# Softmax minus one-hot over 8192 rows: row-wise transfers, hand-placed semaphores, column numbers in PSUM, and middle blocks moved as two transfers of half the partitions

## The chip, the cores and the metric

The kernel runs on one core of a Trainium2 chip. A core has compute engines that run side by side, each with its own instruction queue: TensorE (PE), VectorE (DVE), ScalarE (ACT), GpSimd (POOL) and SyncE (SP). Data moves between HBM (the large memory, in which inputs and outputs lie) and SBUF (the on-chip memory of 128 partitions) by DMA; here SP and ACT issue the transfers, each on a queue of its own. PSUM is a second, small on-chip memory of 128 partitions. The engines wait for each other and for transfers by semaphores.

The metric is the device time of one execution, in microseconds, given as the median of ten runs. Lower is better.

## The reference

The input is 8 x 1024 rows of 8192 float32 logits and one label per row. The output is the gradient of the cross entropy: the softmax of each row, less one at the row's label.

```
logits_max = np.max(logits, axis=-1, keepdims=True)
exp_logits = np.exp(logits - logits_max)
softmax = exp_logits / np.sum(exp_logits, axis=-1, keepdims=True)
one_hot[batch_idx, seq_idx, labels] = 1.0
return (softmax - one_hot).astype(np.float32)
```

268 MB are read and 268 MB written. The arithmetic is a maximum, an exponential with its sum, a scaling, and a compare with a subtraction, each over all elements.

## The kernel before

The 8192 rows are taken as 64 tiles (T) of 128 rows, one row per partition (P). A tile is 128 x 8192 float32, 4 MB, 32 KB in each partition, and is worked on in place. The pool `io` has six such slots (SLOTS).

Ahead of the loop the labels are loaded by ACT's queue (line 44), turned into one label per partition by a cast on DVE (56) and a transpose on PE (58), and written twice by DVE (61), once for each half of the columns (HALF, 4096). GpSimd writes the column numbers 0 to 4095 as int16 into SBUF (`iota`, 46).

Each tile t goes through six steps:

- `load(t)`, line 65: one transfer on SP's queue. It waits until the slot is free, that is for the store of tile t-6.
- `row_max`, line 70, on DVE: the negated maximum of each row, `m`.
- `exponent`, line 75, on ACT: exp(x + m) in place, with the sum `s` of each row.
- `inverse`, line 80, on DVE: `r`, the reciprocal of `s`.
- `normalize`, line 86, on ACT: x times r, as two instructions of 4096 columns.
- `subtract`, line 91, on DVE: x less (column number equals label), as two instructions of 4096 columns. The second half compares with the label less 4096.

and then `store(t)`, line 97: one transfer on ACT's queue.

The order on each engine is that of the program text (`manual_schedule`); the framework places the semaphores. The loop, lines 103 to 112, is skewed: within iteration t, DVE runs the inverse of t, the maximum of t+1 and then the subtract of t, and ACT runs the exponent of t, issues the store of t-1, and scales t. So the subtract of t stands behind the maximum of t+1 on DVE, and the latter waits for the load of t+1. SP carries only loads, and runs ahead as far as slots are free. PE and GpSimd have nothing to do in the loop.

Of the kernel before, what the change touches and what calls it, by code (L numbers as in the profile page):

```python
# [1 line left out]

# [4 lines left out]

P = 128
HALF = 4096
SLOTS = 6  # L10


@with_exitstack
def kernel(
    ctx: ExitStack,
    tc: tile.TileContext,
    logits: bass.AP,
    labels: bass.AP,
    out: bass.AP,
):  # L20
    nc = tc.nc
    fp32 = mybir.dt.float32
    i32 = mybir.dt.int32
    i16 = mybir.dt.int16
    Act = mybir.ActivationFunctionType
    Alu = mybir.AluOpType

    x_nv = logits.flatten_outer_dims()
    o_nv = out.flatten_outer_dims()
    N, V = x_nv.shape  # L30
    T = N // P
    C = V // HALF
    lab_tp = labels.rearrange("a b -> (a b)").rearrange("(t p) -> t p", p=P)

    const = ctx.enter_context(tc.tile_pool(name="const", bufs=1))
    io = ctx.enter_context(tc.tile_pool(name="io", bufs=SLOTS))
    stats = ctx.enter_context(tc.tile_pool(name="stats", bufs=4))
    psum = ctx.enter_context(tc.tile_pool(name="psum", bufs=1, space=bass.MemoryType.PSUM))
    ctx.enter_context(tc.manual_schedule())

    lab_raw = const.tile([T, P], labels.dtype)
    nc.scalar.dma_start(out=lab_raw[:], in_=lab_tp)
    iota = const.tile([P, HALF], i16)
    nc.gpsimd.iota(iota[:], [[1, HALF]], base=0, channel_multiplier=0)  # L46
    ident = const.tile([T, T], fp32)
    nc.gpsimd.memset(ident[:], 0.0)  # L48
    nc.gpsimd.affine_select(  # L49
        out=ident[:], in_=ident[:], compare_op=Alu.not_equal, fill=1.0,  # L50
        base=0, pattern=[[-1, T]], channel_multiplier=1,
    )
    lab_f = const.tile([T, P], fp32)
    lab32 = lab_raw[:].bitcast(i32)
    step = mybir.dt.size(labels.dtype) // 4
    nc.vector.tensor_copy(out=lab_f[:], in_=lab32.rearrange("t (p s) -> t p s", s=step)[:, :, 0])  # L56
    lab_ps = psum.tile([P, T], fp32)
    nc.tensor.transpose(out=lab_ps[:], in_=lab_f[:], identity=ident[:])  # L58
    lab = const.tile([P, C, T], fp32)
    for c in range(C):  # L60
        nc.vector.tensor_scalar_add(out=lab[:, c, :], in0=lab_ps[:], scalar1=float(-c * HALF))  # L61

    def load(t):
        x = io.tile([P, V], fp32, tag="x", name="x")
        nc.sync.dma_start(out=x[:], in_=x_nv[t * P : (t + 1) * P, :])  # L65
        return x

    def row_max(x):
        m = stats.tile([P, 1], fp32, tag="m", name="m")
        nc.vector.tensor_reduce(out=m[:], in_=x[:], axis=mybir.AxisListType.X, op=Alu.max, negate=True)  # L70
        return m

    def exponent(x, m):
        s = stats.tile([P, 1], fp32, tag="s", name="s")
        nc.scalar.activation(out=x[:], in_=x[:], func=Act.Exp, bias=m[:], scale=1.0, accum_out=s[:])  # L75
        return s

    def inverse(s):
        r = stats.tile([P, 1], fp32, tag="r", name="r")
        nc.vector.reciprocal(out=r[:], in_=s[:])  # L80
        return r

    def normalize(x, r):
        for c in range(C):
            xc = x[:, c * HALF : (c + 1) * HALF]
            nc.scalar.activation(out=xc, in_=xc, func=Act.Copy, bias=0.0, scale=r[:])  # L86

    def subtract(t, x):
        for c in range(C):
            xc = x[:, c * HALF : (c + 1) * HALF]  # L90
            nc.vector.scalar_tensor_tensor(  # L91
                out=xc, in0=iota[:], scalar=lab[:, c, t : t + 1], in1=xc,
                op0=Alu.is_equal, op1=Alu.subtract, reverse1=True,
            )

    def store(t, x):
        nc.scalar.dma_start(out=o_nv[t * P : (t + 1) * P, :], in_=x[:])  # L97


    xs, ms = {}, {}  # L100
    xs[0] = load(0)
    ms[0] = row_max(xs[0])
    for t in range(T):
        s = exponent(xs[t], ms[t])
        r = inverse(s)
        if t + 1 < T:
            xs[t + 1] = load(t + 1)
            ms[t + 1] = row_max(xs[t + 1])
        if t > 0:
            store(t - 1, xs[t - 1])  # L110
        normalize(xs[t], r)
        subtract(t, xs[t])
    store(T - 1, xs[T - 1])


# [1 line left out]
_INS = ['logits', 'labels']  # L117
_OUTS = [((8, 1024, 8192), 'float32')]


# [23 lines left out]
```

## Time and profile before

| what | value |
|---|---|
| median of ten runs | 1248.19 us (1248.06 to 1248.61) |
| the profiled execution, its own time | 1248.27 us |
| span of its profile | 1246.4 us |
| load of a tile, issue to landing (median) | 24.2 us |
| store of a tile, issue to landing (median) | 54.9 us |
| maximum of a tile, DVE | 8680 ns |
| exponent of a tile, ACT | 7122 ns |
| scale of half a tile, ACT | 3700 ns |
| subtract of half a tile, DVE | 4476 ns |

The profile is of one execution. Its span is somewhat shorter than the time of the run, which holds what lies before the first and after the last recorded instruction. "Busy" of an engine counts its compute instructions. In the rows, "L70" is line 70 of the kernel, `m<-x` says that `m` is written from `x`, and a name after `<-` at the end of a row is what the engine waited for last. The time from issue to landing includes the time that a transfer stands in its queue behind earlier ones. q1 is the queue of SP's transfers and q10 that of ACT's.

### The profile page before, as it was taken

The numbers are of one execution on the slowest core, as the hardware profiler recorded it, in microseconds if no ns is written. First come the engines' busy times: TensorE is split into PE (matmuls) and PEld (weight loads), VectorE is DVE, ScalarE is ACT, GpSimd is POOL, SyncE is SP. The second block draws the span as 40 slices with busy tenths as digits, with TensorE's granted clock in tenths as the row PEclk, the third lists the DMA queues.
The fourth block names the chain that finished last, engine by engine and source line by source line (L and its number), as shares of the span: only waits on it lengthen the run. The fifth ranks groups of instructions, "written<-read, shape, count | busy, mean of one in ns | idle before, by whom it ended". The sixth has DMA issues, their size and how long they took to land.

```text
span 1246.4 us, 997 instructions
## 1 busy us (share of the span) xinstructions
PE 0.3 (0%) x1; PEld 0.2 (0%) x1; DVE 1122.1 (90%) x259; ACT 930.7 (75%) x257; POOL 4.1 (0%) x7
## 2 busy tenths in 40 slices
PE   0000000000000000000000000000000000000000
PEld 0000000000000000000000000000000000000000
DVE  3999999999988989889898898988989989899893
ACT  3888888888877777777777777677777777777772
POOL 1000000000000000000000000000000000000000
DMA  9999999999999999999999999999999999999998
GB/s 403 424 436 432 428 437 435 432 430 435 435 431 431 435 435 431 430 435 434 432 429 437 432 433 429 437 433 431 431 437 431 433 431 436 433 432 431 436 433 380
DMA packets 18519, 537.00 MB, mean 431 GB/s; under 512 B 2064, under 2 KB 2128, under 8 KB 2128
## 3 DMA queue, kind: packets, MB, share of 16 engines
q1 hardware_dynamic: 9216, 268.44, 50.0%
q10 hardware_dynamic: 9296, 268.51, 49.9%
q14 instruction: 7, 0.06, 0.0%
HBM read 268.50 MB, written 268.44 MB: 431 GB/s over the span
## 4 chain that ended last, share of the span: by engine, by line
another core or an unknown queue 66%; DVE 21%; DMA 7%; issue 3%; SPq 1%; ACT 1%; DVEq 0%; ACTq 0%
DVE m L70 11%; DVE x L91 10%; DMA out_dram<-x 4%; DMA x<-in_logits_dram 3%; SPq L65 1%; ACT x L75 1%; DVEq L139 0%; ACT x L86 0%; DVE r L80 0%; ACTq L97 0%; DVEq L91 0%; DVEq L70 0%
## 5 line engine op out<-in xcount | busy, mean ns | idle before, releaser
L70 DVE TENSOR_REDUCE m<-x 128x1 f32<-128x8192 f32 x64 | 555.5, 8680 | 84.0 <-DMA x<-in_logits_dram 83.9
L75 ACT ACTIVATE x<-x,m 128x8192 f32<-128x8192 f32 x64 | 455.8, 7122 | 157.2 <-DVE m L70 157.2
L91 DVE SCALAR_TENSOR_TENSOR x<-iota,lab,x 128x4096 f32<-128x4096 int16 x128 | 567.7, 4476 | 4.1 <-ACT x L86 4.1
L86 ACT ACTIVATE x<-x,r 128x4096 f32<-128x4096 f32 x128 | 467.6, 3700 | 123.5 <-DVE r L80 123.5
L80 DVE RECIPROCAL r<-s 128x1 f32<-128x1 f32 x64 | 9.9, 155 | 7.3 <-ACT x L75 7.3
L75 ACT ACTIVATION_READ_ACCUMULATOR x<-x,m 128x1 f32 x64 | 12.0, 187 | 0.0
L75 ACT ACT_TABLE_LOAD x1 | 1.3, 1283 | 13.6 <-DMA x<-in_logits_dram 13.6
L56 DVE CAST lab_f<-lab_raw 64x128 f32<-64x128 int32 x1 | 0.2, 219 | 12.3 <-DMA lab_raw<-in_labels_dram 12.3
L46 POOL IOTA iota<- 128x4096 int16 x1 | 3.5, 3540 | 0.4 <-POOLq L128 0.4
L61 DVE TENSOR_SCALAR lab<-lab_ps 128x64 f32<-128x64 f32 x2 | 0.4, 219 | 0.5 <-PE lab_ps L58 0.5
L58 PE MATMUL lab_ps<-ident,lab_f 64*128 64x64 f32 x1 | 0.3, 335 | 12.7 <-DVE lab_f L56 12.7
L49 POOL TENSOR_SCALAR_AFFINE_SELECT ident<-ident 64x64 f32<-64x64 f32 x1 | 0.2, 232 | 0.1
L58 PEld LDWEIGHTS lab_ps<-ident,lab_f 64*128 64x128 f32 x1 | 0.2, 177 | 12.6 <-issue 12.6
L48 POOL MEMSET ident<- 64x64 f32 x1 | 0.1, 144 | 0.0
L128 POOL MEMSET const-bfloat16-1.0<- 128x1 bf16 x1 | 0.1, 106 | 0.0
L128 POOL MEMSET const-uint8-127<- 128x1 uint8 x1 | 0.1, 106 | 0.0
L128 POOL MEMSET const-float32-0.0<- 128x1 f32 x1 | 0.1, 103 | 0.2 <-issue 0.2
L128 POOL MEMSET const-float32-1.0<- 128x1 f32 x1 | 0.1, 103 | 0.0
## 6 DMA issues: line engine op xcount, KB each, us to landing
x<-in_logits_dram SPq DMA_DIRECT2D x64, 4096.0 KB, 24.2
out_dram<-x ACTq DMA_DIRECT2D x64, 4096.0 KB, 54.9
lab_raw<-in_labels_dram ACTq DMA_DIRECT2D x1, 64.0 KB, 11.5
```

What stands on the lines that cost most here:

```text
L46: nc.gpsimd.iota(iota[:], [[1, HALF]], base=0, channel_multiplier=0)
L49: nc.gpsimd.affine_select(out=ident[:], in_=ident[:], compare_op=Alu.not_equal, fill=1.0, base=0, pattern=[[-1, T]], channel_multiplier=1,)
L56: nc.vector.tensor_copy(out=lab_f[:], in_=lab32.rearrange("t (p s) -> t p s", s=step)[:, :, 0])
L58: nc.tensor.transpose(out=lab_ps[:], in_=lab_f[:], identity=ident[:])
L61: nc.vector.tensor_scalar_add(out=lab[:, c, :], in0=lab_ps[:], scalar1=float(-c * HALF))
L65: nc.sync.dma_start(out=x[:], in_=x_nv[t * P : (t + 1) * P, :])
L70: nc.vector.tensor_reduce(out=m[:], in_=x[:], axis=mybir.AxisListType.X, op=Alu.max, negate=True)
L75: nc.scalar.activation(out=x[:], in_=x[:], func=Act.Exp, bias=m[:], scale=1.0, accum_out=s[:])
L80: nc.vector.reciprocal(out=r[:], in_=s[:])
L86: nc.scalar.activation(out=xc, in_=xc, func=Act.Copy, bias=0.0, scale=r[:])
L91: nc.vector.scalar_tensor_tensor(out=xc, in0=iota[:], scalar=lab[:, c, t : t + 1], in1=xc, op0=Alu.is_equal, op1=Alu.subtract, reverse1=True,)
L128: nc = _bacc.Bacc("TRN2", target_bir_lowering=False, num_devices=1)
```

## The change

A new layout of rows: 256 rows are a block, there are 32 blocks (B), and partition p holds rows 2p and 2p+1 of the block (G = 2, index j). So the two rows of a partition lie side by side in HBM, and in SBUF in the tile `X` of three block slots (SLOTS is now 3), as large as the six slots before. One step of the loop still handles 128 rows: row j of each partition.

A block moves in one of three ways, set for each block by the strings LOADS and STORES:

- `r`: two transfers, one for each j, each over all 128 partitions with 32 KB per partition;
- `h`: two transfers, the even partitions and the odd ones, each with both rows, 64 KB per partition;
- `w`: one transfer, all partitions with both rows.

Loads are `r` for block 0, `w` for block 1, `r` for 2 to 6, `h` for 7 to 26 and `r` to the end. Stores are `r` for blocks 0 to 3, `h` for 4 to 23, `r` for 24 to 29, `w` for 30 and `r` for 31. A load of block b waits for those stores of block b-3 that share elements with it. A maximum waits for all transfers that bring part of its row. With `h` or `w`, the store is issued after the second row of the block.

Loads stay on SP's queue and stores on ACT's. The semaphores are placed by hand: the helper `run` gives each instruction its last wait and puts any other wait ahead of it as an instruction of its own. Slots of loads and of stores have semaphores of their own, two per slot. At the end ACT waits for the last stores.

The column numbers 0 to 8191 are written by GpSimd as int16 into what will be the second row of slot 2, and copied by DVE, read as int32, into a PSUM tile[...]. The load of that row (block 2, j = 1) waits for the copy. The label transposes use the same PSUM tile before that. The scale and the subtract take a whole row in one instruction, except for the last tile, whose scale and subtract stay in halves. The order of steps on DVE and ACT in the loop is as before. The statistics `m`, `s` and `r` have a column for each tile instead of rotating buffers.

The diff, cut to its core:

```
-HALF = 4096
-SLOTS = 6
+G = 2
+SLOTS = 3
+LOADS = "rwrrrrrhhhhhhhhhhhhhhhhhhhhrrrrr"
+STORES = "rrrrhhhhhhhhhhhhhhhhhhhhrrrrrrwr"
...
+    x_b = x_nv.rearrange("(b p j) v -> b p j v", p=P, j=G)
+    o_b = o_nv.rearrange("(b p j) v -> b p j v", p=P, j=G)
...
+    X = const.tile([P, SLOTS, G, V], fp32)
...
+    iota = psum.tile([P, V], i16)
+    lab_ps = iota[:].bitcast(fp32)[:, :T].rearrange("p (j b) -> p j b", j=G)
...
+        def run(engine, waits, counter, method, **operands):
+            waits = list(dict.fromkeys(waits))
+            for w in waits[:-1]:
+                engine.wait_ge(*w)
+            instruction = getattr(engine, method)(**operands)
+            for w in waits[-1:]:
+                instruction._wait_ge(*w)
+            step = 16 if method == "dma_start" else 1
+            instruction.then_inc(counter, step)
...
+        made = X[:, SLOTS - 1, G - 1, :].bitcast(i16)[:, :V]
+        w_made = run(
+            nc.gpsimd, [], pool, "iota", out=made, pattern=[[1, V]], base=0, channel_multiplier=0
+        )
...
+        w_iota = run(
+            nc.vector, [w_turned, w_made], dve, "tensor_scalar",
+            out=iota[:].bitcast(i32), in0=made.bitcast(i32), scalar1=0, scalar2=None, op0=Alu.bitwise_or,
+        )
...
+        PIECES = {
+            "r": [(every, slice(j, j + 1)) for j in range(G)],
+            "h": [(slice(i, P, 2), rows) for i in range(2)],
+            "w": [(every, rows)],
+        }
...
+        def load(b):
+            loaded[b] = []
+            before = stored.get(b - SLOTS, last_made if b == SLOTS - 1 else [])
+            for q, piece in enumerate(PIECES[LOADS[b]]):
+                ps, js = piece
+                free = [w for other, w in before if meets(piece, other)]
+                w = run(
+                    nc.sync, free, got[b % SLOTS][q], "dma_start",
+                    out=X[ps, b % SLOTS, js, :], in_=x_b[b, ps, js, :],
+                )
+                loaded[b].append((piece, w))
+        def store(t):
+            b, j = divmod(t, G)
+            stored.setdefault(b, [])
+            for q, piece in enumerate(PIECES[STORES[b]]):
+                ps, js = piece
+                if js.stop != j + 1:
+                    continue
+                w = run(
+                    nc.scalar, [finished[t]], put[b % SLOTS][q], "dma_start",
+                    out=o_b[b, ps, js, :], in_=X[ps, b % SLOTS, js, :],
+                )
+                stored[b].append((piece, w))
...
+            n = 1 if t + 1 < T else 2
+            cols = [slice(i * V // n, (i + 1) * V // n) for i in range(n)]
...
+        store(T - 1)
+        for b in range(B - SLOTS, B):
+            for _, w in stored[b]:
+                nc.scalar.wait_ge(*w)
```

## The prediction

> **What bounds the kernel now.** I read the page first: part 1 for the engines, part 2 for the DMA row, part 3 for the queues, then the waits of the compute engines and of SP, then a table of stages, and last the timeline of one row in the middle and of the end.
>
> ```profile
> PE 0.3 (0%) x1; PEld 0.2 (0%) x1; DVE 1122.1 (90%) x259; ACT 930.7 (75%) x257; POOL 4.1 (0%) x7
> DMA  9999999999999999999999999999999999999998
> GB/s 403 424 436 432 428 437 435 432 430 435 435 431 431 435 435 431 430 435 434 432 429 437 432 433 429 437 433 431 431 437 431 433 431 436 433 432 431 436 433 380
> ...
> q1 hardware_dynamic: 9216, 268.44, 50.0%
> q10 hardware_dynamic: 9296, 268.51, 49.9%
> ```
>
> The sixteen DMA engines are busy in every slice, and queues q1 (loads) and q10 (stores) share their time half and half. VectorE is the next engine with 90%. Is it close enough to be the bound? The stages answer that (columns: stretch, its length, busy time and count of each engine, clock, DMA share, GB/s):
>
> ```profile
> 20.00:60.00 40.00, 0.00 (x0) 0.00 (x0) 32.72 (x9) 33.34 (x9) 0.00 (x0) 1.00 0.99 423
> 60.00:290.00 230.00, 0.00 (x0) 0.00 (x0) 230.00 (x54) 191.71 (x54) 0.00 (x0) 1.00 1.00 433
> 290.00:600.00 310.00, 0.00 (x0) 0.00 (x0) 283.76 (x67) 235.70 (x65) 0.00 (x0) 1.00 1.00 433
> 600.00:900.00 300.00, 0.00 (x0) 0.00 (x0) 272.15 (x62) 223.88 (x63) 0.00 (x0) 1.00 1.00 433
> ...
> 1230.00:1247.00 17.00, 0.00 (x0) 0.00 (x0) 0.25 (x1) 0.00 (x0) 0.00 (x0) 1.00 0.74 318
> ```
>
> From 60 to 290 us VectorE is full and eats the lead of the six loads that were issued at once. The DMA moves 433 GB/s there too, and goes on at 433 when VectorE falls back to 91%. So the rate doesn't depend on who waits for whom. The waits say the same from the other side:
>
> ```profile
> DVE m L70 <- DMA x<-in_logits_dram: 83.9, 46, 2.4
> ```
>
> and, in SP's own list,
>
> ```profile
> SPq L65 <- DMA out_dram<-x: 1149.3, 58, 67.1
> ```
>
> The row maximum waits for loads, and SP's loads wait for stores to free a slot. One row in the middle:
>
> ```profile
> 500.95 8.69 DVE L70 TENSOR_REDUCE m<-x 128x1 f32<-128x8192 f32 x1 [1.80 <-DMA x<-in_logits_dram]
> 509.55 8.87 DVE L91 SCALAR_TENSOR_TENSOR x<-iota,lab,x 128x4096 f32<-128x4096 int16 x2
> ...
> 518.45 0.34 ACTq L97 DMA_DIRECT2D out_dram<-x  x1
> ...
> 520.75 8.69 DVE L70 TENSOR_REDUCE m<-x 128x1 f32<-128x8192 f32 x1 [2.26 <-DMA x<-in_logits_dram]
> ```
>
> VectorE needs 8.69 + 8.87 + 0.16 (the reciprocal) = 17.7 us a row less overlaps, 17.45 in the full stretch. A row in and out is 8.39 MB, at 433 GB/s 19.37 us. All 536.9 MB at 433 are 1240 us of a span of 1246.4. Only 6.4 us lie outside the saturated rate: the start (403 and 424 GB/s in the first two slices) and the drain of the last store (380).
>
> [...] 9216 packets for 64 loads are 8192 data packets of 32 KB plus 16 small ones a transfer. At 433 a wave of sixteen 32 KB packets takes 1210.8 ns[...].
>
> **The change, part by part.**
>
> *Row-wise loads and stores (r) in 12 blocks.* The same 4 MB transfers of 128 pieces of 32 KB, only with a step of 64 KB in DRAM. The same count, the same size: 0. It is bounded below and above by a DRAM effect of the step that no row shows; I take 0, with 0.3% (1 us) either way.
>
> *Whole blocks and half partitions (w, h).* 20 blocks of loads and 20 of stores go as two transfers of 64 partitions, and one load and one store as one transfer of 128. The bytes are 42 of 64 blocks' worth, 65.6%, or 813 of the 1240 us. Two rows of one partition lie side by side in DRAM and in X, so a piece is 64 KB instead of 32 KB, if the DMA takes it whole. [...] If the piece is still cut at 32 KB it is nothing. [...] I take 1.9.
>
> *Fewer slots, coarser.* Three blocks of two rows instead of six rows: the same SBUF. But with h a row can begin only when both halves have landed, and both stores are issued only after the second row. The loop is: a block lands; its first maximum and the previous row's subtract follow; the store of the previous block is issued 17.5 us after the landing (500.95 to 518.45). Then store half 0, load half 0 beside store half 1, load half 1: 3 x 19.4 us while both queues are full. In all 75.7 us of the two block periods, 77.5. Before, the same loop had five row periods, 96.9, for 17.5 + 2 x 19.4 = 56.3. So 40 us of slack shrink to 1.8, and the hand-offs have to fit in there: a load takes 24.2 us from issue to landing by part 6 where its transfer takes 19.4, so 4.8 each. They don't fit. What then? A late load leaves the stores alone, which then go at 9.7 us a transfer instead of 19.4, so the lost time comes back. At full rate the loop is 17.5 + 3 x 9.7 + 3 x 4.8 = 61 us, under 77.5. The DMA loses only when both queues are empty at once. Stepped from a landing at 0, with the store of half 1 8.8 us of work short of its end beside the next load's half 0: shared, it ends at 17.6, the next store is issued at 17.5, and the load has about 1 us left. An idle DMA answers about 1 us after an issue: SP's first is at 0.74 us, and in the DMA view of the first 20 us the first bytes stand in the slice from 1.5 to 2.0. I take no gap. It rests on each half's load waiting for the store of the same half only.
>
> *Whole-row scale and subtract.* ACT's two of 3.70 become one, by the exponent's row (7.12) 0.2 us shorter; VectorE's two become one of about 8.75. The subtract now starts after the whole scale, not after its first half. In the middle the scale ends at 526.15 and the subtract can't start before 529.35, so the cover is 3.2 us; in the full stretch it is 0.8 us (54.75 against 55.59). Cost 0. The last row stays in halves.
>
> *Column numbers in PSUM.* The subtract reads 8192 int16 from PSUM. [...] The bound below is 0 gain; above, VectorE has 19.37 - 8.69 - 0.16 = 10.5 us for it before it becomes the bound. To fill it, VectorE copies 4096 int32 ahead of the first maximum: as long as a half subtract, about 4.4 us. The first maximum starts at 18 instead of 13.51, and the first store is issued at 51.5 instead of 47.04. What hides it is the loads, 25.2 MB, that alone last until about 60 us. Then the two first stores leave a hole of up to a microsecond around 72 us, as the second isn't issued before 69. I take 0.5, between 0 and 1.5.
>
> *Hand-placed semaphores.* Extra waits of half blocks stand on SP, before loads that wait for stores anyway, and on VectorE before a maximum: a few tens of ns against 1.8 us of idle. Behind that maximum wait the subtract and, through it, ACT's store; they waited there before. SP carries nothing but loads, so nothing else is held. 0. The waits at the end on ACT replace those of L139 (SP waits there for the last store): 0, up to 0.5 either way.
>
> Sum: -1.9 + 0.5 = -1.4 on the profiled run of 1248.27 us (span 1246.4 and 1.9 around it), 1246.9. The median, 1248.19, is the same within 0.1: 1246.8 us.
>
> **Rivals.**
> 1. [...] It decides from 0.5% (4 us) on. For it: nothing in before excludes it. [...] 0.13.
> 2. *Both queues run dry in the h loop.* A gap of 1 us per block is 20 us, 1267; 0.2 us decides. For it: the slack of 1.8 against hand-offs of 4.8. Against: the idle queue's answer and the full rate. 0.10, half of it below 1258.
> 3. *VectorE becomes the bound*, with a PSUM read slower by a fifth: each us over 10.5 costs 64 us. 1311. 0.02.
> 4. *The pieces are cut at 32 KB*: only the late start remains, 1248.7. It is in the main case's range.
>
> **How the numbers follow.** The main case, DMA saturated throughout, has 0.75, mostly from 1244.2[...] to 1249.5. A measurement can tell about 0.2%, 2.5 us, from no change. Of the 0.75 I put 0.30 below 1245.7, 0.41 within and 0.04 above 1250.7. With the rivals 0.29 is slower. The range leaves out rival 1, half of rival 2 and rival 3: 1244.2 to 1258; the likeliest case's own is 1244.2 to 1249.5.
>
> **What would show it.** Right: packets fall from 18519 to about 13000; the middle stages read 434 with a DMA share of 1.00; VectorE's subtract is one row of some 8.75 us; the first maximum starts near 18 us. Rival 1: share 1.00 but GB/s well under 433 in the middle only. Rival 2: a share under 1.00 there. Rival 3: VectorE full to the end. Wrong altogether: [...]a shorter start or drain, for which I see no cause.

## The result, and the profile after

The changed kernel takes 1276.61 us (median), the one before 1248.23 us. The ratio is 1.0227, with a 95% interval of 1.0216 to 1.0237: 28 us slower, where 1.4 us faster were forecast. Its runs also scatter more, 1272.9 to 1280.7 us; of the 29 runs before, all but two (1254.0 and 1280.6) lie within 0.8 us. The profiled execution took 1275.87 us with a span of 1273.9, against 1246.4 before.

First the lines of the page that answer to those read before: the DMA row, GB/s in 40 slices, the packets and the two queues.

```profile
DMA  9999999999999999999999999999999999999998
GB/s 397 427 429 437 433 430 444 420 430 430 397 397 428 428 422 430 399 428 428 395 432 391 428 428 424 428 391 430 428 399 426 425 415 430 437 432 429 439 443 372
DMA packets 13076, 536.98 MB, mean 422 GB/s; under 512 B 2032, under 2 KB 2032, under 8 KB 2064
...
q1 hardware_dynamic: 6512, 268.44, 50.4%
q10 hardware_dynamic: 6560, 268.51, 48.8%
```

The pieces did become 64 KB: 13076 packets instead of 18519. But in the middle, where the h blocks are, GB/s dips below 400 in seven slices (11, 12, 17, 20, 22, 27 and 30; a slice is 31.8 us), where before it never fell under 428 there. It comes back to 429 and more when the rows go one by one again (slices 34 to 39). The stages show the same, and what the DMA share says of it (columns as before):

```profile
60.00:290.00 230.00, 0.00 (x0) 0.00 (x0) 209.42 (x37) 173.51 (x37) 0.00 (x0) 1.00 1.00 431
290.00:600.00 310.00, 0.00 (x0) 0.00 (x0) 272.58 (x49) 223.33 (x49) 0.00 (x0) 1.00 0.99 419
600.00:900.00 300.00, 0.00 (x0) 0.00 (x0) 264.36 (x46) 218.47 (x46) 0.00 (x0) 1.00 0.99 416
900.00:1150.00 250.00, 0.00 (x0) 0.00 (x0) 228.72 (x40) 188.97 (x40) 0.00 (x0) 1.00 1.00 425
1150.00:1230.00 80.00, 0.00 (x0) 0.00 (x0) 71.43 (x14) 58.07 (x15) 0.00 (x0) 1.00 1.00 433
```

The rate falls by 3 to 4%, the busy share by only 1%. So engines stand idle a little, and are slow for the rest: two losses, not one. In the waits the maximum is held less often and much longer: 25 times and up to 20.2 us, where it was 46 times and at most 2.4 us.

```profile
DVE m L68 <- DMA X<-in_logits_dram: 106.6, 25, 20.2
ACT X L68 <- DVE r L68: 75.0, 44, 2.1
ACT X L68 <- issue: 73.7, 20, 6.4
```

What decides is in the chain of work that ended last. Its pieces between 563 and 686 us, in order of time (start, length, what):

```profile
563.52 41.66 DMA out_dram<-X
605.18 0.02 issue
605.20 21.52 DMA X<-in_logits_dram
626.72 0.02 issue
626.74 8.69 DVE m L68
635.43 7.32 DVE X L68
642.74 1.26 issue
644.00 0.17 DVE r L68
644.17 0.43 ACTq L68
644.60 0.04 issue
644.64 41.31 DMA out_dram<-X
685.95 0.02 issue
685.96 21.30 DMA X<-in_logits_dram
```

This is the loop of the prediction, closed: the stores of a block, the load into the freed half slot, the first maximum of the block that landed, the subtract of the row before, the next stores. A round takes 644.64 - 563.52 = 81.1 us and carries two blocks each way, for which the DMA needs 77.5 at 433 GB/s. It is the longest of seven in a row; they take 80.2 on average (by their store issues), 2.7 over, and ten such rounds, for 20 blocks, are 27 us. The chain of the kernel before can't be laid beside it: its pieces in the middle are put down to "another core or an unknown queue". The load at 605.20 is issued when the load before it is about to end and the stores have ended. The DMA view of 600 to 620 us (40 slices of half a microsecond) counts a packet where it starts, in both rows, so a 0 alone is no idle engine:

```profile
DMA  9900699006007993000994099990306933039030
GB/s 786 1180 0 0 262 1311 524 0 0 262 0 0 262 1311 393 131 0 0 0 1573 393 131 0 262 262 393 1049 0 131 0 262 1573 131 131 0 131 1835 0 131 0
```

The individual packet records of the trace say how many engines had a packet: 16 until 605.0, 2 at 606.0, 16 again from 607.75. As stages: 321 GB/s from 604 to 614 us, with a share of 0.92. The records also give the two losses a size. A 64 KB packet takes 2.418 us (two of 32 KB took 2 x 1.213), and nine in ten are within 0.1 us of that. The exceptions come in bursts: from 200 to 1050 us, packets that took longer than their kind add 21.6 us to each engine's time, nearly all of them loads (20.1). Most of it comes in eight bursts of some 32 packets (two per engine on average), each of which costs an engine 1.8 to 2.3 us on average, always right behind a load's restart like that at 605; the rest in smaller ones. Engines without a packet add 7.5 us. Together 29.1 us, less 2.7 that the larger packets save (8 ns on each of 5376, spread over 16 engines), against a span longer by 27.5.

### The profile page after: what moved, and what is told of

The parts are those of the page before. It is cut to its first block, busy times and chain, and to the rows that moved or that the text cites. A ratio compares the mean times of both kernels' runs of the same rounds, so it can differ in the third digit from the quotient of the medians.

```text
span 1273.9 us, 629 instructions
## 1 busy us (share of the span) xinstructions
PE 0.4 (0%) x2; PEld 0.3 (0%) x2; DVE 1117.6 (88%) x196; ACT 917.9 (72%) x194; POOL 7.4 (1%) x7
## 2 busy tenths in 40 slices
DMA packets 13076, 536.98 MB, mean 422 GB/s; under 512 B 2032, under 2 KB 2032, under 8 KB 2064
## 3 DMA queue, kind: packets, MB, share of 16 engines
q10 hardware_dynamic: 6560, 268.51, 48.8%
## 4 chain that ended last, share of the span: by engine, by line
DMA 61%; DVE 34%; ACT 1%; issue 1%; ACTq 1%; DVEq 0%; PE 0%; SPq 0%
DMA out_dram<-X 38%; DMA X<-in_logits_dram 23%; DVE m L68 17%; DVE X L68 16%; ACT X L68 1%; ACTq L68 1%; DMA lab_raw<-in_labels_dram 0%; DVE iota L68 0%; DVEq L56 0%; DVE r L68 0%; DVE lab_f L68 0%; PE iota L68 0%; DVE lab L68 0%; ACTq L220 0%; DVEq L67 0%
## 5 line engine op out<-in xcount | busy, mean ns | idle before, releaser
L68 DVE TENSOR_REDUCE m<-X 128x1 f32<-128x8192 f32 x64 | 555.1, 8674 | 106.6 <-DMA X<-in_logits_dram 106.6
L68 ACT ACTIVATE X<-X,m 128x8192 f32<-128x8192 f32 x64 | 455.6, 7119 | 188.3 <-DVE m L68 188.2
L68 DVE SCALAR_TENSOR_TENSOR X<-iota,lab,X 128x8192 f32<-128x8192 int16 (+1 forms) x65 | 559.7, 8612 | 22.2 <-ACT X L68 22.2
L68 ACT ACTIVATE X<-X,r 128x8192 f32<-128x8192 f32 (+1 forms) x65 | 456.0, 7016 | 148.7 <-DVE r L68 75.0
L68 ACT ACTIVATION_READ_ACCUMULATOR X<-X,m 128x1 f32 x64 | 11.9, 186 | 0.0
L68 POOL IOTA X<- 128x8192 int16 x1 | 6.9, 6943 | 0.0
L68 DVE TENSOR_SCALAR iota<-X 128x4096 int32<-128x4096 int32 x1 | 4.4, 4428 | 0.1
```

Source lines behind the costliest of these rows:

```text
L68: instruction = getattr(engine, method)(**operands)
```

## Experiments

Two theories at first. A: the h transfers make the loss, either because both queues run dry (A1; "dry" is used here for engines without a packet) or because an h transfer is slow of itself (A2). B: something else in the change costs.

**All blocks row by row (e1).**

```
-LOADS = "rwrrrrrhhhhhhhhhhhhhhhhhhhhrrrrr"
-STORES = "rrrrhhhhhhhhhhhhhhhhhhhhrrrrrrwr"
+LOADS = "r" * 32
+STORES = "r" * 32
```

> The changed kernel with every block moved row by row (r), loads and stores. Theory A (the h transfers make the whole loss): about 1248.5 us, within 1 us of the kernel before, DMA share 1.00 and 433 GB/s in the middle. Rival B (something else in the change costs: column numbers in PSUM, the late first maximum, hand-placed waits): 1255 us or more, with the same dips of GB/s in the middle.

1248.09 us, ratio 0.9995 (0.9988 to 1.0003). B is out: PSUM, whole-row instructions, hand-placed waits and the row layout together neither cost nor bring anything that can be measured. All of the loss is in w and h.

**Early stores, with h (e2) and with r (e3).** In both, the subtraction is gone and the store follows its own scale:

```
-            if t > 0:
-                store(t - 1)
...
-            for c, w in zip(cols, scaled):
-                w = run(nc.vector, [w], dve, "scalar_tensor_tensor", ...)
-            finished.append(w)
-        store(T - 1)
+            finished.append(scaled[-1])
+            store(t)
```

> The changed kernel with its h blocks, but the subtraction of the one-hot is left out and each store is issued right behind its scale on ACT, some 19 us earlier after the landing of the block; so the store queue should never run dry. Theory A1 (both queues run dry at the hand-over; the restart of all engines together is what makes the h loads slow, and a mixed stream of h transfers is as fast as before): 1244 to 1248 us, 433 to 434 GB/s in the middle, share 1.00. Rival A2 (an h transfer is slow of itself, whenever loads run, and this makes the loop late): 1262 us or more, with the middle under 428 GB/s at a share of 1.00.

> The same early stores without the subtraction, but all blocks r: the yardstick for the run before. Both theories: 1245 to 1248 us, 433 GB/s. Under A1 the run before is level with this or up to 3 us faster (larger packets); under A2 it is at least 15 us slower than this.

h 1259.99 us (1258.37 to 1267.25), r 1247.82 us. Both A1 and A2 miss: more than half of the loss is gone, and 12 us are left. The stages of the h run:

```profile
290.00:600.00 310.00, 0.00 (x0) 0.00 (x0) 140.99 (x32) 227.39 (x49) 0.00 (x0) 1.00 1.00 430
600.00:900.00 300.00, 0.00 (x0) 0.00 (x0) 132.22 (x31) 227.65 (x48) 0.00 (x0) 1.00 1.00 431
```

No idle share, and before the last stores next to no idle engine in its records (0.02 us from 60 to 1235 us), but 430 instead of 433, from single slow loads scattered over the stream (8.3 us in all after the first 60 us). The rest is at the end: the last slice of its page reads 336 GB/s against 391 in the r twin, and from 1200 us on its engines stand idle for 7.9 us against 3.3. The slow packets are no steady price of h: from 505 to 570 us and from 735 to 800 the stream runs at 433 GB/s. So there are several costs, and the dry queues are the largest.

**Contiguous halves (e4).**

```
-            "h": [(slice(i, P, 2), rows) for i in range(2)],
+            "h": [(slice(i * P // 2, (i + 1) * P // 2), rows) for i in range(2)],
```

> The changed kernel with h as partitions 0 to 63 and 64 to 127 instead of even and odd ones. Theory A1[...] a load alone runs near 217 GB/s, packets of 64 KB take near 4.8 us there, and the whole is 1350 us or more. Rival C (the slow restart comes from HBM[...]): the restart is no slower than with even and odd partitions, 1265 to 1285 us.

1658.56 us (one run). The middle:

```profile
290.00:600.00 310.00, 0.00 (x0) 0.00 (x0) 185.82 (x32) 146.14 (x31) 0.00 (x0) 1.00 1.00 281
```

The engines are busy throughout (a share of 1.00) and move 281 GB/s. Where loads are alone, the records show about 210 GB/s (213 from 293 to 323 us, with packets of some 5 us), half of 433. The 217 GB/s of the expectation was the author's estimate, half of 433; the run bears the figure out and doesn't show what halves the rate. Loads of even and odd partitions run at 434 GB/s where they are alone in the change (279 to 295 us), so an h load is not slow of itself. The bytes and the packets (13076) are those of the change; the other choice of partitions, and of rows with it, costs 382 us. So the forecast of Rival C (1265 to 1285 us) failed. But the run says nothing on why a restart with even and odd partitions is slow, and how the rows of a transfer are spread over the engines it doesn't show either.

**Whole blocks in place of halves (e5)**, LOADS and STORES with w where the change has h. Each transfer then covers all 128 partitions, as a row transfer does, and in the rows-only twin above (e3) such transfers had next to no slow packets (0.06 us of excess from 60 to 1240 us). The hand-over is coarser.

> The changed kernel with w (one transfer of all 128 partitions, 64 KB each) where it has h, [...]but a load waits for the whole store of its slot. Theory A (two costs: queues that run dry[...]): packets of 64 KB stay at 2.42 us, none slow, but the DMA share falls to 0.97 or less in the middle and the whole is 1270 to 1310 us. Rival[...]: share 1.00 and about 1247 us.

1319.28 us, ratio 1.0567 (1.0553 to 1.0582), slower than forecast. The middle stage, and the DMA from 614 to 634 us:

```profile
600.00:900.00 300.00, 0.00 (x0) 0.00 (x0) 242.82 (x43) 200.70 (x42) 0.00 (x0) 1.00 0.95 395
```

```profile
DMA  0099000000993000393006900099000990000099
```

The share falls to 0.95: the dry stretches don't need halves, and the rival's 1247 us is out. Both sides run dry 19 times, and in 18 of them no engine at all has a packet for 1.3 to 1.4 us (the records; in this view the first packets start at 619). But one part of the expectation fell: there are slow packets here as well. In each restart the first wave of sixteen takes 3.0 to 3.2 us instead of 2.42, and a later one, the last before the store queue sets in, 3.4 to 3.7: together some 1.8 us, as in the bursts of the change. So those bursts don't need halves of the partitions. They come with a queue that starts: the first on an empty DMA, the second on one that the other queue has kept full. The kernel before shows both at its start, with packets of 32 KB: its first load loses some 0.65 us, and its first store (48.8 us) costs the loads some 0.5 us. Why the packets are slow then is not shown; the cause that Rival C names is not excluded.

**One side only.**

```
e6: STORES = "r" * 32        (loads as in the change)
e7: LOADS = "r" * 32         (stores as in the change)
e8: STORES = "r" * 32, LOADS with w in place of h
```

> Loads as in the change (h in the middle), stores row by row: the first row's store leaves a row earlier, so the store queue holds out. Theory A: share 1.00 in the middle, no dry stretch[...]: 1253 to 1262 us. Rival A1[...]: 1246 to 1248 us.

> Stores as in the change (h in the middle), loads row by row. Theory A: [...]both stores of a block still leave together after its second row and a row's load waits for both: dry stretches, share 0.97 to 0.99 in the middle, 1255 to 1290 us. Rival A2 (the whole loss is that h loads are slow): 1248 us.

> Loads as w where the change has h, stores row by row: packets of 64 KB on the load side[...], and stores as early as before. Theory A: share 1.00, 433 to 434 GB/s, no slow packets: 1246 to 1248 us, level with or up to 2 us below the kernel before. Rival (a coarse load alone starves the queues): 1255 us or more.

e6 1250.03 us, ratio 1.0015 (1.0008 to 1.0021); e7 1315.47 us (1308 to 1324), above the range that was expected; e8 1247.93 us, ratio 0.9995 (0.9987 to 1.0003). Coarse loads alone are nearly free, though e6 lies between the ranges of its two theories (A: some loads are slow without a dry stretch too; A1: only behind one); coarse stores alone are worse than the change. The chain of e6:

```profile
562.44 24.35 DMA out_dram<-X
...
587.37 35.23 DMA X<-in_logits_dram
...
622.62 8.69 DVE m L68
631.30 7.32 DVE X L68
...
640.00 24.17 DMA out_dram<-X
```

A round is 640.00 - 562.44 = 77.6 us: what the DMA needs, no more. The one store on the chain is of 4 MB and takes 24 us from issue to landing, where the change has both halves issued together and the second lands after 41.7. With the first row's store gone a row earlier, the path has slack, and waits for the DMA and not the other way round. The 1.8 us that e6 is above before go with its few slow packets (2.6 us of excess after the first 60 us, 2.3 of it loads). e8, with whole blocks, is level with before. That is as far as larger packets go: they are there (15460 packets), 0.3 us below before in the median, which is inside the interval.

**Early stores with whole blocks (e9).** Same edit as in the early-store runs, w for h.

> As the h run with early stores and no subtraction, but with whole blocks (w) on both sides: packets of 64 KB[...]. Theory P (what the h run with early stores still lost, 12 us against its r twin[...]): 1245 to 1249 us, hardly a slow packet. Rival Q (64 KB packets on both queues cost by themselves): 1255 us or more with slow packets as there.

1301.56 us (1289 to 1307): by its time this is Rival Q's forecast, but it doesn't tell the two apart, since whole blocks run dry even so (seven times in the records; 405 GB/s at a share of 0.97 from 290 to 600 us). From 545 to 575 us both queues carry 64 KB packets without a slow one; but the h run with early stores has such stretches too (433 GB/s from 505 to 570 us), so this doesn't speak for P either, which put the 12 us down to the halves.

**Small packets (e10).** 64 bytes of padding behind each row split an h piece in two.

```
-    X = const.tile([P, SLOTS, G, V], fp32)
+    X = const.tile([P, SLOTS, G, V + 16], fp32)
...
```

> The changed kernel with 64 bytes of padding behind each row in SBUF, so that an h transfer moves its two rows as pieces of 32 KB instead of 64 KB; all else, the halves and their waits too, is as in the change. Theory S (the hand-over is late [...]): the loop gets some 3 us shorter per two blocks, so most dry stretches go: 1250 to 1262 us. Rival (the halves and the coarse stores alone set it): 1270 to 1280 us as with the change, plus up to 2 us for the smaller packets.

1267.06 us (1260.84 to 1270.63), between the two: a third of the loss goes with the size of the packets. 18452 packets. There is no moment any more with four or fewer engines at work, of which the change has six, and idle engines cost 3.0 us instead of 7.5, but bursts behind the hand-overs are there still (16.6 us of excess). The loop got shorter by some 0.6 us (79.6 on average), not by the 3 that the author had estimated, so that the size acts through the hand-over, as Theory S has it, is not shown.

**A shorter loop (e11, with padding e12).** The first maximum of each block over a quarter of the columns, alone and with the padding:

```
-                out=m[:, t : t + 1], in_=row(t), axis=mybir.AxisListType.X, op=Alu.max, negate=True,
+                out=m[:, t : t + 1], in_=row(t)[:, : V // 4 if j == 0 else V], axis=mybir.AxisListType.X, op=Alu.max, negate=True,
```

> The changed kernel, all transfers as they are, but the maximum of each block's first row is taken over 2048 of its 8192 columns (6.5 us less between the landing of a block and the issue of the previous block's stores; the softmax itself doesn't depend on which shift is used). Theory L (the loop from landing to landing, 80.7 us for two blocks in the trace of the change, is longer than the 77.5 us that the DMA needs, and that alone runs the queues dry): the loop gets to 74 us, no dry stretches, no bursts of slow loads at their ends, 1250 to 1260 us (what the mixed h stream loses[...] is left). Rival (the dry stretches come from the transfers, not from the compute between them): 1270 us or more.

> The same short maximum in the kernel with padded rows (h as pieces of 32 KB). Theory L: nothing is left to gain from the shorter hand-over once the loop has room, so this is within 3 us of the run before, 1250 to 1260 us. Rival (packets of 64 KB cost by themselves when both queues have them): 5 us or more below the run before.

e11 1286.01 us (four runs: 1266.27, 1276.53, 1295.50 and 1296.37), e12 1255.28 us (1254.18 to 1259.72). With padding the loop's length did what was said: 12 us less than e10, by an estimated 6.5 us less on VectorE's path (three quarters of the maximum's 8.67). A round is 77.5 us now, what the DMA needs, and e10's was 79.6. Its stages split in two, here from 200 to 550 us and after:

```profile
200.00:550.00 350.00, 0.00 (x0) 0.00 (x0) 246.88 (x53) 245.63 (x53) 0.00 (x0) 1.00 1.00 426
550.00:1000.00 450.00, 0.00 (x0) 0.00 (x0) 334.87 (x70) 335.41 (x71) 0.00 (x0) 1.00 1.00 433
```

First scattered slow loads, then 433 GB/s with two slow packets in 450 us, with the same even and odd halves. An h stream can thus run at the full rate; what changed at 550 us is not shown. Without padding the expectation for e11 failed as a whole:

```profile
200.00:350.00 150.00, 0.00 (x0) 0.00 (x0) 94.10 (x20) 88.39 (x20) 0.00 (x0) 1.00 0.95 383
350.00:600.00 250.00, 0.00 (x0) 0.00 (x0) 178.90 (x38) 183.56 (x39) 0.00 (x0) 1.00 1.00 430
600.00:900.00 300.00, 0.00 (x0) 0.00 (x0) 219.79 (x47) 217.62 (x47) 0.00 (x0) 1.00 1.00 428
```

From 350 us on it is as Theory L has it: no dry stretch, a share of 1.00, at most one small burst of slow stores per block (0.3 to 0.6 us). From 350 to 1050 us idle engines and slow packets take 8 us together, in the change 25, with the same transfers. But the switch from rows to halves, 200 to 350 us, lost 17 us (150 us at 383 instead of 433) in the profiled run, so that the whole is as slow as the change. The times of the other three suggest that this varies; they have no profile. Why that switch is so costly there is open. The median of e12 lies at least 11 us below each run of e11, where Theory L gave 3 at most and its rival (packets of 64 KB on both queues cost by themselves) 5 or more: on this the rival was right, at the switch at least.

## Why the prediction was wrong

The first reading was right: DMA bounds the kernel before, at 433 GB/s, and with blocks moved by rows the compute engines don't move it (1247.82 us without the subtraction). Point by point:

- *Row-wise layout, PSUM, whole rows, hand-placed semaphores at nothing:* right, by the run with all rows (1248.09 us). The subtract from PSUM takes 8.74 us a row; the 8.75 was the author's estimate, as no row of before reads a long tile there. The "few tens of ns" of a wait were an estimate too; the shortest wait instruction on SP took 27 ns in the kernel before.
- *The late start, 0.5 us:* wrong. VectorE's copy into PSUM takes its 4.43 us, but the labels land at 7.3 instead of 12.3 us (part 6 of the two pages has 6.4 and 11.5 us from issue to landing, now for 32 pieces of 2 KB instead of 64 of 1 KB), so the first maximum starts at 13.58 us, as before at 13.51.
- *Larger packets, -1.9 us:* the gain was the author's estimate, which the packets of one size, 32 KB, in the kernel before couldn't show. In the change the packets are as large as assumed and are 8 ns shorter per 64 KB, which is 2.7 us in all. With loads alone enlarged (e8) the half of it that was due, about 1 us, came out as 0.3, not told from nothing.
- *"I take no gap":* this is the step that failed. The loop was set up with the right members, and its slack of 1.8 us was seen. The argument that lost time comes back, because a queue left alone goes at twice the speed (in the kernel before, stores alone moved 437 GB/s from 1200 to 1230 us, both queues together 433), holds only as long as one queue has something left. It was stepped through from one chosen state, in which the store ended just as the next was issued. In the trace the second store half takes 41.7 us from issue to landing where the sum had 38.8, and the load half behind it 21.5 where it had 19.4; with the 17.9 us from landing to issue that is 81.1 us in place of 75.7, and 80.2 on average over the rounds. So the load that ends a round is issued when the DMA has all but run empty.
- *The cost of a gap.* Rival 2 (0.10) is what came about, by the sign that the prediction gave for it, a share under 1.00 in the middle (0.99). It priced 1 us per block at 20 us, from the idle time alone. The idle time is only 7.5 us; the slow packets behind it cost more, 1.8 to 2.3 us a time; so the DMA loses not only when both queues are empty. No row of before was read for that, though its first load shows a part: its first sixteen packets took 1.5 to 2.1 us instead of 1.21 (the records).
- *Rival 1, a lower rate with half the partitions (0.13):* contiguous halves did move about 210 GB/s where loads were alone (e4), but with even and odd ones little is lost: the loads-only run (e6) is 1.8 us above before. Its 0.13 was the author's estimate; no row of before bore on it.

The length of a round is the loss told over again, so it proves nothing by itself. What settled it is what shortens the round and takes the loss with it: stores row by row with all else as in the change (e6: 77.6 us a round, loss 1.8 us), and less work between landing and issue with the same transfers (e12 against e10: 77.5 and 79.6 us a round, loss 7 and 19 us; e11 against the change from 350 us on: 8 and 25 us lost). What stays open: the cost of the switch in e11, why packets are slow when a queue starts, and how much 64 KB packets on both queues cost by themselves (behind the switch at most the 8 us of e11).

## What to carry to other kernels

When transfers of both directions share one saturated DMA, count the time of the loop from landing to landing against the bytes that it carries, with each transfer's issue-to-landing time from the profile, and don't count on slack of a few per cent (here 1.8 of 77.5 us): making stores coarser cost more here (e7, 1315.47 us) than making loads coarser (e6, 1250.03 us), since the first part of a store waits for the last part of the work. Once rows are 32 KB, larger pieces brought nothing that could be measured here (0.3 us of 1248), so there was nothing to pay the loss of slack with.

## What was not expected of the hardware

- A DMA that had run empty didn't start at its rate: the first wave of sixteen 64 KB packets took 3.0 to 3.2 us instead of 2.42, and another wave, the last before the second queue set in, 3.4 to 3.7 (e5).
- Loads of 64 neighbouring partitions moved about 210 GB/s when alone (e4), loads of every second partition 434 (the change, 279 to 295 us). With stores beside them the latter reached 433 too, but in e12 only after some 350 us at 426.
- The second of two h stores issued back to back holds ACT's queue: in the change the pair takes 1.1 to 4.5 us to issue (a store of a row 0.34), and ACT's scale behind it waited 73.7 us in all ("issue" in the waits). Behind ten of the twenty pairs VectorE's subtract waited for the scale, 1.8 us on average, but in eight of these the maximum after it waited 6.2 to 8.9 us for the next landing anyway.
